# Hybrid decoder block on one core: x loaded first by SP, w_in tiles asked for at the fifth step, both copies of the transposed x on ScalarE

## The chip, the core and the metric

The kernel runs on one core of a Trainium2 chip. Its time is the device time of one execution in microseconds (us); three runs of the kernel before are given. TensorE (PE) multiplies, VectorE (DVE) and ScalarE (ACT) do elementwise work and copies out of PSUM, GpSimd (POOL) sets memory and issues a few DMAs, SyncE (SP) only issues DMAs. Each engine has one queue and works through it in order.

## The reference

One decoder block over 256 tokens of width 2048, in float32:

```
mod = silu(c) @ W_ada + b_ada            # shift1, scale1, gate1, shift2, scale2, gate2
h   = RMSNorm(x) * (1 + scale1) + shift1
u, q, k, v = split(h @ W_in)             # 1024 columns each
y_ssm = GLU(gelu(S5(u)))                 # diagonal complex state space model, 64 groups x 16 channels
y_att = dilated_attention(qk_norm(q, k), v)   # 8 heads of 128, three branches
x = x + gate1 * (concat(y_ssm, y_att) @ W_out)
h2 = RMSNorm(x) * (1 + scale2) + shift2
x = x + gate2 * ((silu(h2 @ W_gate) * (h2 @ W_up)) @ W_down)
```

Only the first part matters here: the norm of x, the modulation, h and the product with the columns of u and the first half of q.

## The kernel before

The 256 tokens are two tiles of 128. Weights come from memory in tiles of 128 x 1024 floats (512 KB), laid out on the host. The products run in two parts for accuracy: each weight tile `raw` is rounded by ScalarE to `whi` (L134), VectorE takes the rest `wlo` = raw - whi (L136), the activations are split likewise, and TensorE adds three products (L153, L630). There are six `raw` buffers and three pairs of `whi` and `wlo`. The tiles of the products follow one list, `order`; `ahead(n)` asks for tiles until n are ready, `take()` for one when none is.

The instructions of SP are issued in the order in which the program writes them. The order of the other engines is worked out by a planner: it goes by the place in the program (earlier is preferred), by priorities written into the code (`tc.high_priority`), and by its own estimate of when operands are there. What it has fixed then runs in order.

At the start three streams are written together in a loop over n (L690). `ada_stream` (L222) computes shift1 and scale1 for 256 columns at a time: a set of eight n has two modulation steps, each of which loads four tiles of W_ada (two into `raw`, two into spare buffers called `rawp`) and multiplies them on TensorE with silu(c). When a set is complete, `ada_finish` (L206) adds its parts by small matmuls and `make_h` (L606) forms h for the two column blocks and puts 10 units of work (`u_units`, L622) in a list: the product of h with two w_in tiles for u (into the accumulators `uacc`) and one for q. From n = 9 on the loop takes units from the list.

`start()` (L650) is the third stream: `x_norm` (L325) and `s5_consts` (L372). `x_norm` transposes x on TensorE through the two accumulators `uacc` (first 8 of the 16 column blocks, then the other 8), copies them to SBUF as `xT` (L340; one accumulator on ScalarE, the other on VectorE), sums squares on ScalarE (L337) and forms the root on VectorE; its result is spread over the partitions by L351. `s5_consts` is a chain of small VectorE operations (powers of the state space matrix); it needs only the small constants `smt` until its last steps, which need `bct`, loaded at n = 10. Behind it come rotations and tables (`ssm_rot`, `ssm_tables`), which `tab_step` takes in portions from n = 9 on.

The small constants and x are loaded by ScalarE's queue (L83, L86), before its first activation; SP loads all weights (L109, L248). `ahead(NHL)` with NHL = 3 asks for the first three w_in tiles at n = 8, after the loads of the third modulation step (the steps begin at n = 0, 4, 8, ..., and are counted from 0 here).

After this come the products for q, k, v with the attention and the state space model between them, W_out, and the feed-forward part, where TensorE works nearly without a break.

Of the kernel before, what the change touches and what calls it, by code (L numbers as in the profile page):

```python
# [60 lines left out]
def body(tc, sm, tabs, bc, brow, x, wada, wg2, win, wglu, wout, wgate, wup, wdown, out):  # L61
    nc = tc.nc
    V, A, PE, G, SP = nc.vector, nc.scalar, nc.tensor, nc.gpsimd, nc.sync
# [11 lines left out]
    def acc(shape, name="acc"):  # L75
        return acc_p.tile(shape, F32, name=name, tag="acc", bufs=2)

    def ms(shape, name="ms"):
        return ms_p.tile(shape, F32, name=name, tag="ms", bufs=3)
# [3 lines left out]
    A.dma_start(smt, sm)  # L83
    xt = [xp.tile([128, D], F32, name=f"x{t}", tag="x", bufs=2) for t in range(2)]
    for t in range(2):
        A.dma_start(xt[t], x[t])  # L86
    col = lambda n: smt[:, COLS[n][0]:COLS[n][1]]
    ident = col("id")
    ones = const.tile([128, 128], F32, name="ones")
# [2 lines left out]
    def rsqrt(pool_, v, n, tag):  # L92

        y = pool_.tile([128, n], F32, name="rsy" + tag)
        t = pool_.tile([128, n], F32, name="rst" + tag)
        V.tensor_scalar(out=y.bitcast(I32), in0=v.bitcast(I32), scalar1=1, scalar2=None, op0=ALU.arith_shift_right)
        V.tensor_scalar(out=y.bitcast(I32), in0=y.bitcast(I32), scalar1=-1, scalar2=0x5F3759DF, op0=ALU.mult, op1=ALU.add)
        for _ in range(3):
            V.tensor_tensor(out=t, in0=y, in1=y, op=ALU.mult)
            V.tensor_tensor(out=t, in0=t, in1=v, op=ALU.mult)  # L100
            V.tensor_scalar(out=t, in0=t, scalar1=-0.5, scalar2=1.5, op0=ALU.mult, op1=ALU.add)
            V.tensor_tensor(out=y, in0=y, in1=t, op=ALU.mult)
        return y
# [20 lines left out]
    def ahead(n, place=None):  # L124
        while len(ready) < n and order:
            raw = load(order.pop())
            if place:
                hl = place([128, 2, 2, 512], "whl", F32R)
                hi, lo = hl[:, 0], hl[:, 1]
            else:  # L130
                hi = ring.tile([128, 2, 512], F32R, name="whi", bufs=NHL)
                lo = ring.tile([128, 2, 512], F32R, name="wlo", bufs=NHL)
            with tc.high_priority(offset=HP):
                A.copy(hi, raw)  # L134
            with tc.high_priority(offset=HP2):
                V.tensor_tensor(out=lo, in0=raw, in1=hi.bitcast(F32), op=ALU.subtract)  # L136
            ready.append((hi, lo))
# [187 lines left out]
    def x_norm():  # L325

        ss1 = p1.tile([128, 2], F32, name="ss1")
        for h in range(2):
            xn = P8([128, 8, 256], f"xT{h}")
            for t in range(2):  # L330
                for i in range(2):
                    for k in range(4):
                        kc = h * 8 + i * 4 + k
                        PE.transpose(uacc[i][:, k, t * 128:(t + 1) * 128], xt[t][:, kc * 128:(kc + 1) * 128], ident)
                if h == 0:
                    junk = P8([128, D], "junk")
                    A.activation(junk, xt[t], AF.Square, accum_out=ss1[:, t:t + 1])  # L337
                    yield
            for i in range(2):
                (V.tensor_copy if i else A.copy)(xn[:, 4 * i:4 * i + 4], uacc[i])  # L340
            xnT.append(xn)
            yield
            if h == 0:
                with tc.high_priority(offset=HH):
                    V.tensor_scalar(out=ss1, in0=ss1, scalar1=1.0 / D, scalar2=EPS, op0=ALU.mult, op1=ALU.add)
                    rs1 = rsqrt(p1, ss1, 2, "a")
                    rb = ms([128, 256], "rb")
                    for t in range(2):
                        dg = T2([128, 128], "dgx")
                        V.tensor_scalar(out=dg, in0=ident, scalar1=rs1[:, t:t + 1], scalar2=None, op0=ALU.mult)  # L350
                        PE.matmul(rb[:, t * 128:t * 128 + 128], lhsT=ones, rhs=dg, start=True, stop=True)  # L351
                    A.copy(rsx, rb)
                yield
# [243 lines left out]
    uacc = [acc([128, 4, 256], f"uacc{i}") for i in range(2)]  # L597
# [44 lines left out]
    def unit():  # L642
        while units:
            try:
                next(units[0])
                return
            except StopIteration:
                units.pop(0)

    def start():  # L650
        a, b = x_norm(), s5_consts()
        while next(a, 0) is None:
            next(b, None)
            yield
        yield
        yield from b

    def tabs_early():
        yield from st_
        for m in range(NTAB):  # L660
# [4 lines left out]
            yield from ssm_tables(m)  # L665

    st_ = start()
    tab_gen = tabs_early()
    U_ = []
# [13 lines left out]
    def tab_step(budget):  # L683
        debt[0] = max(debt[0] - budget, -budget)
        if debt[0] < 0:
            c_ = next(tab_gen, None)
            debt[0] += c_ or 0.0

    work = 0.0
    for n in range(66):  # L690
        next(ada)
        if n == NBC:
            SP.dma_start(bct.rearrange("p a b c -> p (a b c)"), bc)
        if n < 9:
            next(st_)
        else:
            tab_step(TB)
        if n == 8:
            ahead(NHL)
        if n >= U0:  # L700
            work += RATE
            while work >= 1.0:
                unit()
                work -= 1.0
# [552 lines left out]
def program(arrays):  # L1257
    import concourse.bacc as bacc
    nc = bacc.Bacc("TRN2", target_bir_lowering=False, num_devices=1)
    aps = {k: nc.dram_tensor(k, v.shape, F32, kind="ExternalInput").ap() for k, v in arrays.items()}  # L1260
    out = nc.dram_tensor("out", (2, 128, D), F32, kind="ExternalOutput").ap()
    with tile.TileContext(nc) as tc:
        body(tc, out=out, **aps)
    return nc
# [8 lines left out]
```

## Time and profile before

| | |
|---|---|
| median of 3 runs | 1247.62 us (1245.65 to 1249.0) |
| profiled execution | 1249.01 us, span 1247.2 us |
| busy: TensorE, VectorE, ScalarE, GpSimd | 1195.1, 789.7, 570.5, 50.4 us |
| granted TensorE clock, mean | 0.991 |
| read from memory | 301.54 MB, 245 GB/s over the span |

Busy times are sums over one profiled execution; TensorE's are modelled, so that a busy TensorE isn't one at its peak. A wait counts only when something that ends late depends on it. Times in rows are microseconds from the start of the span.

### The profile page before, as it was taken

The page shows a single profiled execution, that of the slowest core. Times are in us where ns is not written, and L with a number is a line of the kernel's source. Part 1 is how long each engine was busy: PE and PEld are TensorE (multiplying, and loading weights), DVE is VectorE, ACT ScalarE, POOL GpSimd, SP SyncE. Part 2 cuts the span into 40 slices and gives each one's busy share as a digit, 9 for nine tenths or more (in the row PEclk, how much of TensorE's full clock was granted, in tenths as well). Part 3 has the DMA queues.
Part 4 walks back from the last instruction along what each step waited for, and adds up shares of the span by engine and source line. Part 5 has one row for each costly group of instructions (what it writes and reads, how often), then busy time and mean ns, then how long its engine had stood idle before and what let it go on. Part 6 is the DMA issues. An engine that isn't in the chain of part 4 may idle for free.

```text
span 1247.2 us, 16987 instructions
## 1 busy us (share of the span) xinstructions
PE 1195.1 (96%) x6312; PEld 954.0 (76%) x6312; DVE 789.7 (63%) x1370; ACT 570.5 (46%) x871; POOL 50.4 (4%) x90
## 2 busy tenths in 40 slices
PE   4889899999998999999999999999999999999998
PEld 2667667667798777688888888888888878888886
DVE  7964666577879988856665565565555444545544
ACT  3654574456455545544444444444444443434332
POOL 1110001121020000000000000000000000000000
PEclk9899999999999999999999999999999999999999
DMA  9879878897996899367777777777765656666662
GB/s 378 315 288 365 312 275 292 274 315 262 339 301 215 309 319 337 117 208 240 236 236 233 233 240 244 225 235 249 236 189 186 195 161 200 206 197 206 199 205 68
DMA packets 93906, 306.85 MB, mean 246 GB/s; under 512 B 18080, under 2 KB 20544, under 8 KB 93184
## 3 DMA queue, kind: packets, MB, share of 16 engines
q1 hardware_dynamic: 80784, 294.69, 70.5%
q0 software_dynamic: 11312, 6.70, 2.8%
q10 hardware_dynamic: 1728, 4.38, 0.9%
q8 instruction: 49, 0.80, 0.3%
q14 instruction: 33, 0.27, 0.1%
HBM read 301.54 MB, written 4.19 MB: 245 GB/s over the span
## 4 chain that ended last, share of the span: by engine, by line
PE 84%; DVE 8%; DMA 3%; ACT 3%; issue 1%; POOL 0%; DVEq 0%; ACTq 0%; POOLq 0%
PE ff L153 38%; PE dn L153 14%; PE qkv L153 8%; PE dnl L153 5%; PE wo L153 4%; PE ada L254 3%; PE uacc L630 2%; DVE wlo L136 2%; DMA raw<-wada 1%; PE wol L153 1%; DMA raw<-win 1%; PE y L754 1%; PE S L724 1%; ACT whi L134 1%; PE q L153 1%
## 5 line engine op out<-in xcount | busy, mean ns | idle before, releaser
L136 DVE TENSOR_TENSOR wlo<-raw,whi 128x1024 fp32r<-128x1024 f32 x365 | 446.0, 1223 | 327.1 <-ACT whi L134 325.8
L134 ACT CAST whi<-raw 128x1024 fp32r<-128x1024 f32 x365 | 384.0, 1054 | 490.9 <-PE ff L153 270.3
L153 PE MATMUL ff<-whi,h2T 128*128 128x512 f32 x1408 | 437.3, 390 | 1.6 <-ACT h2T L1066 1.0
L153 PEld LDWEIGHTS ff<-whi,h2T 128*128 128x128 f32 x1408 | 264.0, 188 | 57.8 <-ACT h2T L1066 1.9
L153 PE MATMUL ff<-wlo,h2T 128*128 128x512 f32 x704 | 274.0, 389 | 0.0
L153 PE MATMUL dn<-whi,aT 128*128 128x512 f32 x528 | 163.2, 390 | 0.0
L153 PEld LDWEIGHTS ff<-wlo,h2T 128*128 128x128 f32 x704 | 132.2, 188 | 27.1
L153 PEld LDWEIGHTS dn<-whi,aT 128*128 128x128 f32 x528 | 99.1, 188 | 21.0 <-ACT whi L134 0.2
L153 PE MATMUL qkv<-whi,hT 128*128 128x512 f32 x320 | 108.2, 405 | 0.3 <-ACT whi L134 0.3
L153 PE MATMUL dn<-wlo,aT 128*128 128x512 f32 x264 | 103.1, 391 | 0.0
L153 PEld LDWEIGHTS qkv<-whi,hT 128*128 128x128 f32 x320 | 60.6, 190 | 25.5 <-issue 7.3
L1125 DVE SCALAR_TENSOR_TENSOR gate<-raw,cs,gate 128x1024 f32<-128x1024 f32 x32 | 41.1, 1285 | 47.1 <-DMA raw<-wg 47.1
L153 PE MATMUL qkv<-wlo,hT 128*128 128x512 f32 x160 | 64.0, 400 | 2.0 <-DVE wlo L136 2.0
L630 PE MATMUL uacc<-hT,whi 128*128 128x256 f32 x256 | 53.1, 304 | 7.0 <-ACT whi L134 7.0
L153 PEld LDWEIGHTS dn<-wlo,aT 128*128 128x128 f32 x264 | 49.6, 188 | 10.8 <-issue 0.5
L153 PE MATMUL dnl<-whi,aT 128*128 128x512 f32 x176 | 54.4, 389 | 0.0
L630 PEld LDWEIGHTS uacc<-hT,whi 128*128 128x128 f32 x256 | 43.2, 207 | 13.6 <-ACT whi L134 10.0
L254 PE MATMUL ada<-raw,c 128*4 128x256 f32 (+1 forms) x496 | 50.5, 489 | 0.0
L284 DVE SCALAR_TENSOR_TENSOR gate<-raw,cs,gate 128x1024 f32<-128x1024 f32 x32 | 41.0, 1282 | 8.6 <-DMA raw<-wada 8.2
L630 PE MATMUL uacc<-hT,wlo 128*128 128x256 f32 x128 | 39.4, 308 | 5.8 <-DVE wlo L136 5.8
L153 PEld LDWEIGHTS dnl<-whi,aT 128*128 128x128 f32 x176 | 33.0, 188 | 7.0 <-DVE o L359 0.2
L153 PEld LDWEIGHTS qkv<-wlo,hT 128*128 128x128 f32 x160 | 30.4, 190 | 9.0 <-DVE wlo L136 2.4
(318 smaller groups left out, 1253.5 us busy)
## 6 DMA issues: line engine op xcount, KB each, us to landing
raw<-wada SPq DMA_DIRECT2D x130, 512.0 KB, 5.3
raw<-wgate SPq DMA_DIRECT2D x88, 512.0 KB, 4.3
raw<-wup SPq DMA_DIRECT2D x88, 512.0 KB, 4.2
raw<-wdown SPq DMA_DIRECT2D x88, 512.0 KB, 3.6
raw<-win SPq DMA_DIRECT2D x64, 512.0 KB, 5.4
raw<-wout SPq DMA_DIRECT2D x32, 512.0 KB, 4.9
raw<-wg SPq DMA_DIRECT2D x32, 512.0 KB, 4.2
rawp<-wada SPq DMA_DIRECT2D x30, 512.0 KB, 7.4
```

The source lines that it names most:

```text
L134: A.copy(hi, raw)
L136: V.tensor_tensor(out=lo, in0=raw, in1=hi.bitcast(F32), op=ALU.subtract)
L153: PE.matmul(ps[t] if type(ps) is list else ps[:, t], lhsT=lhs(a, t), rhs=w[:, j], start=first and n == 0, stop=last and n == 2)
L254: PE.matmul(ps[32 * q:32 * q + 4, 0:w], lhsT=c7[:, kc, 3 - i:7 - i], rhs=wts[t][:, j * w:(j + 1) * w], start=q not in seen, stop=n == len( ...
L284: V.scalar_tensor_tensor(out=gb, in0=wt, scalar=cs[:, k:k + 1], in1=gb, op0=ALU.mult, op1=ALU.add)
L630: PE.matmul(uacc[b][:, c], lhsT=wt[:, j, w], rhs=h[:, j, a], start=(kc == 0 and n == 0 and c % 2 == 0), stop=(kc == 15 and n == 2), skip_g ...
L724: PE.matmul(S[:, e, Q], lhsT=wv[:, 0, Q, e].rearrange("p i c -> p (i c)"), rhs=U[:, m, Q], start=True, stop=True)
L754: PE.matmul(y[:, Q], lhsT=Vt[:, Q, e].rearrange("p r c -> p (r c)"), rhs=hp[:, e, Q], start=False, stop=e == 1, skip_group_check=True)
L1125: V.scalar_tensor_tensor(out=g, in0=wt, scalar=cs[:, k:k + 1], in1=g, op0=ALU.mult, op1=ALU.add)
```

## The change

Three edits in the code before the loop and one in it. SP issues the two loads of x, ahead of everything else in its queue; ScalarE issues only the small constants. Both copies of the transposed x are on ScalarE. In `start()` the steps of `s5_consts` no longer alternate with `x_norm` throughout: two of its steps are taken at n = 0 and 1, none from n = 2 to 8, the rest from n = 9 on by `tab_step`. Before, one was taken at each n from 0 to 4 and from 6 to 8. `ahead(NHL)` stands at n = 4, behind the loads of the second modulation step.

```
     for t in range(2):
-        A.dma_start(xt[t], x[t])
+        SP.dma_start(xt[t], x[t])
...
             for i in range(2):
-                (V.tensor_copy if i else A.copy)(xn[:, 4 * i:4 * i + 4], uacc[i])
+                A.copy(xn[:, 4 * i:4 * i + 4], uacc[i])
...
     def start():
         a, b = x_norm(), s5_consts()
-        while next(a, 0) is None:
-            next(b, None)
+        for i in range(9):
+            next(a, None)
+            if i < 2:
+                next(b, None)
             yield
-        yield
         yield from b
...
-        if n == 8:
+        if n == 4:
             ahead(NHL)
```

## Rows read from the trace of the kernel before

**Rows 1.** The page's chain of work that ended last: shares by engine.
```profile
PE 84%; DVE 8%; DMA 3%; ACT 3%; issue 1%; POOL 0%; DVEq 0%; ACTq 0%; POOLq 0%
```

**Rows 2.** Windows by stage: window, busy us (instructions) per engine, clock, DMA share, GB/s.
```profile
0.00:40.00 40.00, 20.73 (x166) 14.59 (x167) 31.49 (x193) 13.88 (x24) 5.79 (x17) 0.92 0.98 385
40.00:100.00 60.00, 51.85 (x494) 38.72 (x494) 43.49 (x129) 35.79 (x84) 8.17 (x11) 0.94 0.78 283
100.00:160.00 60.00, 54.98 (x520) 40.57 (x519) 35.56 (x93) 29.02 (x58) 2.01 (x6) 1.00 0.90 347
160.00:200.00 40.00, 39.47 (x242) 27.55 (x242) 27.29 (x74) 26.20 (x68) 0.42 (x1) 1.00 0.81 289
550.00:1247.00 697.00, 692.58 (x3091) 572.27 (x3089) 376.50 (x331) 282.67 (x283) 0.00 (x0) 1.00 0.67 210
```

**Rows 3.** Timeline of TensorE, 10 to 50 us: start, length, instruction, wait before it.
```profile
15.06 1.89 PE L254 MATMUL ada<-rawp,c 128*4 128x256 f32 x16 [2.79 <-DVE ss_tb L362]
...
21.51 1.75 PE L334 MATMUL uacc<-smt,x 128*128 128x128 f32 x14 [1.32 <-DVE xT L340]
23.20 1.05 PE L254 MATMUL ada<-rawp,c 128*4 128x256 f32 x16
24.06 1.05 PE L254 MATMUL ada<-raw,c 128*4 128x256 f32 x16
...
27.93 1.05 PE L254 MATMUL ada<-raw,c 128*4 128x256 f32 x16
30.61 0.51 PE L630 MATMUL uacc<-hT,whi 128*128 128x256 f32 x2 [1.64 <-ACT whi L134]
33.98 0.58 PE L630 MATMUL uacc<-hT,wlo 128*128 128x256 f32 x1 [2.86 <-DVE wlo L136]
...
46.00 1.05 PE L254 MATMUL ada<-raw,c 128*4 128x256 f32 x16
```

**Rows 4.** Timeline of VectorE, 19 to 85 us.
```profile
20.23 1.22 DVE L340 COPY xT<-uacc 128x1024 f32<-128x1024 f32 x1 [3.20 <-PE uacc L334]
...
32.70 1.22 DVE L136 TENSOR_TENSOR wlo<-raw,whi 128x1024 fp32r<-128x1024 f32 x1
```

**Rows 5.** Windows in the first 70 us, columns as in Rows 2 (engines PE, PEld, DVE, ACT, POOL).
```profile
0.00:5.00 5.00, 0.00 (x0) 0.00 (x0) 0.89 (x5) 1.28 (x1) 3.88 (x15) 1.00 0.66 196
5.00:40.00 35.00, 20.73 (x166) 14.59 (x167) 30.60 (x188) 12.60 (x23) 1.90 (x2) 0.90 1.02 412
35.00:40.00 5.00, 5.00 (x25) 5.00 (x25) 4.74 (x12) 1.00 (x5) 0.00 (x0) 0.50 1.03 410
40.00:50.00 10.00, 8.28 (x72) 6.05 (x71) 9.65 (x29) 4.43 (x16) 1.84 (x2) 0.99 0.60 216
20.00:70.00 50.00, 39.41 (x362) 29.15 (x361) 48.43 (x202) 28.13 (x68) 4.59 (x6) 0.90 0.88 340
```

**Rows 6.** Timeline of SP's queue, 0 to 130 us.
```profile
17.86 7.20 SPq L109 DMA_DIRECT2D raw<-win  x3
...
28.98 0.90 SPq L248 DMA_DIRECT2D rawp<-wada  x2
...
37.56 9.44 SPq L109 DMA_DIRECT2D raw<-wada  x2
```

**Rows 7.** The tile x, to 60 us: ns min/median/max, first and last start.
```profile
L86 ACTq DMA_DIRECT2D x<-x x2: 354/402/450, 1.2 to 5.3; - x2
L337 ACT ACTIVATE junk<-x x2: 1910/1911/1912, 10.2 to 14.0; 128x2048 f32<-128x2048 f32 x2
...
DMA to landing us min/median/max: 8.7/8.8/9.0
```

**Rows 8.** The tile xT, to 60 us: columns as in Rows 7.
```profile
L340 ACT COPY xT<-uacc x2: 1012/1012/1012, 19.7 to 23.1; 128x1024 f32<-128x1024 f32 x2
L340 DVE COPY xT<-uacc x2: 1223/1224/1224, 20.2 to 26.4; 128x1024 f32<-128x1024 f32 x2
```

**Rows 9.** Timeline of ScalarE, 0 to 100 us.
```profile
29.53 2.92 ACT L134 CAST whi<-raw 128x1024 fp32r<-128x1024 f32 x3
```

**Rows 10.** The tile rawp, to 60 us: time to landing.
```profile
DMA to landing us min/median/max: 4.7/8.3/13.9
```

## The prediction

> **What bounds the kernel now.** I read the chain of waits first: TensorE holds 84% of it [rows 1], so time is lost or won where TensorE stands still. The windows by stage say where that is [rows 2]: of the first 40 us TensorE works 20.73, of the next 60 it works 51.85, of the 60 after that 54.98. That is 19.3 + 8.2 + 5.0 = 32.5 us of standing still in the first 160 us, against 4.4 us in the last 697. The change touches only the start, so I read the first 70 us engine by engine.
>
> TensorE [rows 3]: modulation step 0 (32 matmuls) starts at 15.06; the transposes of the second half of x's columns then wait 1.32 us for VectorE's copy of the first; step 1's matmuls stand behind them and end at 24.06 + 1.05 = 25.11, step 2's at 28.98. The first unit of u starts at 30.61, stops after two matmuls and waits 2.86 us for the low part of a w_in tile, so that it really runs from 33.98. Step 3's matmuls stand behind all the units of the first set and end at 46.00 + 1.05 = 47.05.
>
> VectorE [rows 4, 5]: idle for 3.20 us until 20.23, because the copy of uacc stands in its queue and waits for TensorE; from 20 to 70 us it is 97% busy (48.43 of 50). What it could have done at 17 us it drags behind it up to 70.
>
> DMA [rows 5, 6]: 196 GB/s in the first 5 us, then at its ceiling up to 40 us (share 1.02, 412 GB/s), then 0.60 of it up to 50. The SP queue says why: the second of the two loads issued from 37.56 could not go before 37.56 + 9.44 = 47.0, when step 3's matmuls end and free its raw buffer.
>
> **The change part by part.**
>
> *x on SP, first.* Now ScalarE issues the two tiles of x at 1.2 and 5.3 us, and each takes 8.7 to 9.0 us to land, because SP's loads share the DMA engines; the squares that wait for them start at 10.2 and 14.0 [rows 7]. Afterwards SP issues both at some 0.7 to 1.6 us with nothing of its own ahead of them. With 185 KB of small constants, 384 KB of tables and 2,048 KB of x that is 2.68 MB, 0.98 MB of them in the first 5 us and the rest at 412 GB/s: x is complete at 5 + 4.1 = 9 us instead of 14. The price is that the tiles of steps 0 and 1 stand behind 2 MB more. At the end of step 1 it is no price: the same 6,713 KB (6.87 MB) have to arrive by then in either order, 0.98 + 5.89 MB, so 5 + 14.3 = 19.3 us. SP's two more issues cost 0.35 to 0.45 us each [rows 7], hidden because the DMA engines are the ceiling; without that cover, 0.8 us.
> The Trainium skill (DMA: Bandwidth & Descriptors, section Issuing engines are not separate DMA queues) says that transfers issued by different engines end on the same 16 DMA engines and interleave, so that another issuer saves only the issue time. The share of 1.02 agrees with the sharing. By this rule alone x would come as late as now, and the 3.9 us of step 1 below would fall out of the sum: 1245, the time of the first rival; I think it counts less here, because the order of the issues changes too.
>
> *Both copies on ScalarE.* VectorE loses two copies of 1.22 us [rows 8] and the wait of 3.20: 5.6 us. ScalarE gains two copies of 1.01 us, in series where they were side by side, so each pair ends 0.8 us later than it could (2.0 against 1.2). ScalarE's squares of 1.91 us then end at about 11, the copies at 13, the second pair at 17, all before step 1's tiles at 19.3; that wait hides them. Without that cover: 0.8 us a pair, 1.6.
>
> *What is late next: step 1's matmuls.* Today they wait behind transposes that wait for VectorE; then only for their tiles: 19.3 + 1.9 (32 matmuls, 23.20 to 25.11) = 21.2 against 25.11, **3.9 us** earlier. From there to the first unit of u it is 5.5 us today (25.11 to 30.61: copy of the sums, small matmuls, g and shift, h); I leave that: 26.7.
>
> *w_in tiles at the fifth step.* Three tiles, 1.57 MB, go ahead of step 2's 2.1 MB and land by 19.3 + 3.8 = 23.1. ScalarE's casts (three in 2.92 us [rows 9]) and the first subtraction (1.22 us [rows 4]) then end by 26 to 27, so the stop from 30.61 to 33.98 goes: **3.4 us**. Bounds: 0 if the subtractions stay behind the constants in VectorE's queue, 3.4 if they come ahead of them; I take 3.4, as VectorE has 3.2 us more room. Step 2's tiles land 3.8 us later, at about 28; its matmuls end at 28.98 today, so nothing is lost while the first unit runs ahead of them.
>
> *Six steps of the state space constants* move from steps 2 to 8 to step 9 and later, and with them the rotations and tables in the order in which the planner prefers work. They need only the small constants, so VectorE still has nothing better before 20 us; I cost it at nothing. Bounds: a gain of 1 us if a subtraction that now comes before them saves TensorE another wait, a loss of 3.2 if VectorE idles as it does now.
>
> **The sum.** Two chains run through the first 70 us, and the later one counts: TensorE's first unit is 3.9 + 3.4 = 7.3 us earlier, VectorE's backlog 5.6. TensorE's small matmuls for the tables wait for VectorE, so part of the 7.3 is given back; I take the middle, 6.5. The DMA engines must follow: they idle 10 x 0.40 = 4.0 us in 40 to 50 and 60 x 0.22 = 13.2 in 40 to 100 [rows 2, 5]; with step 3's matmuls some 7 us earlier the raw buffer comes free in time and the first of these gaps closes. From 160 us TensorE's queue is nearly full (39.47 of 40 us), so the lead is carried to the end. The profiled execution took 1249.01 us, its span 1247.2 and 1.8 around it: 1249.0 - 6.5 = 1242.5. The median of the runs, 1247.62, is 1.4 below it: **1241.1 us**.
>
> **The clock.** From 35 to 40 us the granted clock is 0.50 [rows 5], after TensorE had stood from 31.1 to 33.98, so the first unit ran at 1.2 GHz. I assume the same afterwards, since TensorE stands between 21.2 and 26.7.
> The Trainium skill (TensorE: Matmul & The Clock Gate, Part 1) says that an array that idles falls to 1.2 GHz and has to be kept busy to rise again; the 0.50 after the stop agrees. By it an earlier start after a longer pause could keep the first unit slow for longer than now, and the gain would be 1 to 3 us less, an estimate inside the range.
>
> **Rivals.**
> *The lead is swallowed.* From 100 to 160 us the DMA engines are 0.90 busy at 347 GB/s [rows 2]. If the loop of buffer, load and matmul between 50 and 100 us keeps its idle time, only the gap at 45 us counts, and part of it: 2 to 3 us, 1245. For: the high share. Against: the 13.2 us of idle DMA time ahead of it, more than the lead needs. If a raw buffer holds the third early w_in load, so that the change does not do all it says, two of three still come and it ends here too. Chance 0.22.
> *The lead grows.* Casts and subtractions of the second and third set come ahead of the table work, and TensorE's 8.2 us of waits in 40 to 100 us shrink too: lead 10 to 14 us, 1237 to 1233. For: step 3's last tiles were issued by 28.98 + 0.90 [rows 6] and used after 45. Against: VectorE has the same work less 2.4 us. Chance 0.16.
> *Slower: step 2 blocks the first unit.* There are six raw buffers: four go to steps 0 and 1, so with three w_in tiles ahead, step 2's second tile needs one that step 1's matmuls free, and SP issues in order. Step 2's matmuls stand ahead of the first unit now. If they stay there, it waits for their tiles: issued from 21.2, landed 8.3 us later [rows 10], 1.9 us of matmuls, 31.4, still before 33.98. It turns into a loss when they are issued after 33.98 - 1.9 - 8.3 = 23.8. With step 1 ending at 25.11 as now it is 35.3, 1.3 us later, and a hole of some 3 us in the load stream besides, with step 3 behind it: 1247.6 + 4.3 = 1252. For: SP's third w_in load waits like this today, until 17.86 + 7.20 = 25.06 [rows 6]. Against: x is there 5 us sooner, so nothing holds step 1 so long. Chance 0.16.
>
> **How the numbers follow.** Forecast (lead of 4 to 9 us) 0.46, swallowed 0.22, grows 0.16, slower 0.16. About 0.3% (3.7 us) is what a measurement of this kernel tells from no change: faster 0.46 + 0.16 = 0.62, the same 0.22, slower 0.16. The range goes from the grown lead (1233) to most of the slower case (1251).
>
> **What would show it.** Right: the second tile of x landed by 10 us; VectorE without its wait at 17 to 20; step 1's matmuls over by 22; the first unit running from 26 to 28 without a stop for the low part; no DMA gap at 43 to 48; TensorE's work at 200 us 5 to 8 us earlier. Wrong: step 2's matmuls ahead of the first unit and it at 33 or later, or a lead at 60 us that is gone by 160.

## The result, and the profile after

The changed kernel takes 1255.86 us (median of 6 runs, 1252.96 to 1256.39), the kernel before 1247.96 beside it (6 runs). The ratio is 1.0055 [1.0039, 1.0071]: slower by 6.9 us [4.9, 8.9] (the medians lie 7.9 apart). 1241.1 was predicted, 6.5 us faster.

Where it is lost can be read from the start of the feed-forward part, which is the same work in both. From the tile `ff` (ns of one: least, median, most; first and last start), first of the kernel before, then of the changed one:

```profile
L153 PE MATMUL ff<-whi,h2T x1408: 387/389/504, 507.4 to 998.2; 128*128 128x512 f32 x176
```

```profile
L153 PE MATMUL ff<-whi,h2T x1408: 387/389/504, 514.6 to 1005.4; 128*128 128x512 f32 x176
```

It starts 7.2 us later and ends 7.2 later; the spans differ by 7.3 (1247.2 and 1254.5). The first unit of u starts 5.8 us later (30.61 in [rows 3], where it stops again until 33.98; 36.43 below, where it runs on), the last matmul of u 7.9 us later (165.4 and 173.3). So the loss is made in the first 165 us and carried on. The windows of the changed kernel, as in [rows 2]:

```profile
0.00:40.00 40.00, 17.73 (x118) 12.98 (x119) 33.21 (x200) 16.86 (x31) 5.79 (x17) 0.89 0.87 338
40.00:100.00 60.00, 50.22 (x476) 37.09 (x475) 38.15 (x112) 31.02 (x64) 5.42 (x7) 0.93 0.84 304
100.00:160.00 60.00, 52.86 (x531) 39.67 (x529) 34.66 (x98) 30.02 (x68) 4.64 (x10) 1.00 0.87 317
160.00:200.00 40.00, 39.48 (x253) 27.09 (x252) 26.53 (x71) 25.86 (x67) 0.42 (x1) 1.00 0.79 283
```

TensorE works 3.00 us less in the first stretch, 1.63 less in the second, 2.12 less in the third and the same in the fourth: 6.75 of the 7.3.

TensorE's timeline from 14 to 62 us, changed kernel, beside [rows 3]:

```profile
20.71 1.22 PE L351 MATMUL rb<-dgx,ones 128*128 128x128 f32 x4 [4.10 <-DVE dgx L350]
21.87 1.89 PE L254 MATMUL ada<-rawp,c 128*4 128x256 f32 x16
23.53 1.40 PE L254 MATMUL ada<-raw,c 128*4 128x256 f32 x16
...
25.62 1.04 PE L254 MATMUL ada<-raw,c 128*4 128x256 f32 x16
27.16 0.61 PE L211 MATMUL adac<-sel,adaev 128*128 128x2 f32 x4 [0.50 <-ACT adaev L266]
36.43 0.80 PE L630 MATMUL uacc<-hT,whi 128*128 128x256 f32 x2 [8.66 <-ACT hT L616]
42.00 1.05 PE L254 MATMUL ada<-rawp,c 128*4 128x256 f32 x16
...
58.47 0.80 PE L630 MATMUL uacc<-hT,whi 128*128 128x256 f32 x2 [4.31 <-ACT whi L134]
```

Three waits are new. `rb`, which spreads the root of x's norm, now stands ahead of step 0's matmuls; step 0, which ran at 15.06, waits behind it. Step 1 ends at 26.66 (before 25.11). The sums of the modulation are out at 27.77, but h comes 8.66 us later. And the second unit waits 4.31 us for a cast.

Why h is late stands in VectorE's timeline, 23 to 56 us:

```profile
29.60 1.29 DVE L359 TENSOR_TENSOR wkr<-te,el 128x512 f32<-128x512 f32 x2
30.93 0.76 DVE L359 TENSOR_TENSOR te<-wkr 128x256 f32<-128x256 f32 x2
31.61 2.35 DVE L136 TENSOR_TENSOR wlo<-raw,whi 128x1024 fp32r<-128x1024 f32 x2
33.88 0.15 DVE L215 TENSOR_TENSOR sh<-adac,smt 128x2 f32<-128x2 f32 x1
...
35.36 0.88 DVE L614 SCALAR_TENSOR_TENSOR htmp<-xT,g,rsx 128x256 f32<-128x256 f32 x2
```

It is hardly ever idle, but it works on the powers (`el`), the first rotation (`wkr`, `te`) and two low parts before it comes to the shift. In the trace 187 of its instructions start ahead of the shift, in the kernel before 135 (the expectations below count them in the instruction list, as 177 and 128).

What step 0's delay does to the loads: SP's queue, and windows of the changed kernel (columns as in [rows 5]).

```profile
11.27 13.63 SPq L109 DMA_DIRECT2D raw<-win  x3
25.00 1.93 SPq L109 DMA_DIRECT2D raw<-wada  x2
```

```profile
20.00:25.00 5.00, 4.29 (x44) 2.11 (x48) 5.00 (x48) 2.32 (x3) 0.00 (x0) 1.00 0.36 143
25.00:30.00 5.00, 2.27 (x36) 1.08 (x28) 4.90 (x34) 1.42 (x2) 0.00 (x0) 1.00 0.89 293
30.00:35.00 5.00, 0.00 (x0) 0.00 (x0) 4.93 (x10) 0.00 (x0) 0.00 (x0) 0.61 1.03 415
35.00:40.00 5.00, 3.57 (x14) 3.38 (x15) 4.82 (x10) 3.90 (x16) 0.00 (x0) 0.50 1.00 409
```

The third w_in load can't be issued before 11.27 + 13.63 = 24.90, when step 0's matmuls end and free its raw buffer. The DMA engines, at their ceiling there before [rows 5], fall to 0.36. TensorE does nothing from 30 to 35; the granted clock falls to 0.61 and then 0.50 (1.2 GHz), as it did before after the stop at 31. (The 1.00 of the window from 20 to 25 is not a measured clock; the last section says why.)

Of what was meant, x comes early. Tile x of the changed kernel, beside [rows 7]:

```profile
L337 ACT ACTIVATE junk<-x x2: 1894/1902/1911, 6.8 to 10.0; 128x2048 f32<-128x2048 f32 x2
...
DMA to landing us min/median/max: 5.8/7.3/8.8
```

### The profile page after: what moved, and what is told of

Same layout as the page of the kernel before. It is cut to its first block, busy times and chain, and to the rows that moved or that the text cites. A ratio compares the mean times of both kernels' runs of the same rounds, so it can differ in the third digit from the quotient of the medians.

```text
span 1254.5 us, 16980 instructions
## 1 busy us (share of the span) xinstructions
PE 1196.6 (95%) x6312; PEld 955.9 (76%) x6312; DVE 787.7 (63%) x1368; ACT 573.3 (46%) x873; POOL 50.3 (4%) x90
## 4 chain that ended last, share of the span: by engine, by line
PE 85%; DVE 6%; DMA 3%; ACT 3%; issue 1%; SPq 0%; POOL 0%; DVEq 0%; POOLq 0%; ACTq 0%
PE ff L153 38%; PE dn L153 14%; PE qkv L153 7%; PE dnl L153 5%; PE wo L153 4%; PE uacc L630 3%; PE ada L254 3%; DMA raw<-wada 2%; DVE wlo L136 1%; PE q L153 1%; PE wol L153 1%; PE y L755 1%; PE S L725 1%; PE atp L1148 1%; ACT whi L134 1%
```

## The experiments

Four theories, not exclusive: A, VectorE's fixed order holds back the shift and so the first unit. B, TensorE's fixed order (`rb` ahead of step 0) holds a raw buffer, SP and the loads. C, the small constants, on which VectorE's chain starts, come later beside x's loads. D, formed from the first twelve, the fixed start order has a loss of its own at the second unit. The numbers are those in the labels of the runs. Intervals are 95%; a difference of two ratios is good to about 0.2%. The starts of the first unit and of the last matmul of u (uacc) come from one profiled execution each, which can lie some microseconds from its kernel's median (17: 1248.32 and 1251.53; 9: 1259.77 and 1255.47); `wtp` is the tables' first transpose on TensorE. In the kernel before, in 14 and in 15 the first unit stops again, until 33.98, 33.69 and 33.17; in the others it runs on, with 0.8 us of waiting at most.

| kernel | ratio to before | first u | first wtp | last uacc |
|---|---|---|---|---|
| before | 1 | 30.6 | 48.8 | 165.4 |
| changed | 1.0055 [1.0039, 1.0071] | 36.4 | 73.4 | 173.3 |
| x on SP alone (1) | 1.0025 [1.0014, 1.0037] | 38.1 | 53.1 | 170.2 |
| w_in early alone (2) | 0.9998 [0.9983, 1.0014] | 29.9 | 47.4 | 164.2 |
| copies alone (14) | 0.9980 [0.9969, 0.9990] | 29.3 | 48.0 | 162.8 |
| start order alone (15) | 1.0034 [1.0020, 1.0047] | 29.8 | 71.0 | 169.6 |
| all but x on SP (3) | 1.0018 [1.0006, 1.0031] | 28.9 | 68.8 | 166.9 |
| all but w_in early (4) | 1.0033 [1.0021, 1.0044] | 34.6 | 69.6 | 169.1 |
| all but start order (17) | 1.0024 [1.0009, 1.0038] | 36.6 | 52.9 | 168.9 |
| copies and w_in early (18) | 1.0012 [0.9999, 1.0024] | 28.8 | 47.6 | 165.3 |
| both order edges (11) | 1.0003 [0.9991, 1.0016] | 27.9 | 65.8 | 166.5 |
| both, constants on SP (12) | 0.9989 [0.9975, 1.0004] | 27.9 | 65.5 | 164.2 |

**1 to 4: the parts.** Each is the diff above, cut to the part named, or with the part taken out.

*1.* Only `A.dma_start(xt[t], x[t])` to `SP.dma_start(xt[t], x[t])`.

> Only the loads of x go to SP, first; the other three edits are undone. Theory A (order): with x ahead of the modulation tiles in one queue the planner believes that set 0 is complete later and puts some 50 more VectorE instructions ahead of its shift and g (177 instead of 128 stand ahead of them); VectorE works through them in order, so the first unit of u starts late. It expects this edit alone to cost most of the loss: 4 to 8 us slower than before, first unit at 35 us or later. Theory B (buffer): the loss comes from the early w_in loads, the third of which holds SP until 24.9 us and empties the DMA queues; it expects this kernel to be no slower than before, within 2 us. Theory C (small constants landing 1.4 us later, behind x): 1 to 2 us slower.

1.0025, with 185 of VectorE's instructions already ahead of the shift. x on SP alone costs 3.1 us [1.7, 4.6]: the late first unit (38.1) is as A expected, the size is below its 4 to 8 us.

*2.* Only `if n == 8:` to `if n == 4:` ahead of `ahead(NHL)`.

> Only the w_in tiles are asked for at n = 4. Theory A: the order on VectorE stays (127 instructions ahead of the first shift) and the wlo subtractions come earlier, so the first unit loses its stop: 2 to 5 us faster than before. Theory B: the third w_in load waits for a raw buffer and holds SP with step 2's tiles behind it: 3 to 7 us slower, a DMA hole before 30 us. Theory C: no change.

0.9998. The stop for the low part is gone and the first unit starts at 29.9, yet the time is that of before: neither A's gain nor B's loss.

*3.* The change with `SP.dma_start(xt[t], x[t])` back to `A.dma_start`.

> All of the change but the loads of x, which ScalarE issues as before. Theory A: the loss is gone, 0 to 5 us faster than the kernel before. Theory B: the loss stays, 4 to 8 us slower than before, because the early w_in loads are in it. Theory C: the loss shrinks by 1 to 2 us only.

1.0018, which fits none of the three: x takes most of the loss with it, but something is left that isn't the early loads, which are free alone.

*4.* The change with `if n == 4:` back to `if n == 8:`.

> All of the change but the w_in tiles, which are asked for at n = 8 as before. Theory A: still 4 to 8 us slower than before, because shift and g of set 0 stand behind 176 VectorE instructions as in the changed kernel. Theory B: the loss is gone, within 2 us of before. Theory C: 1 to 2 us slower than before.

1.0033, 4.1 us [2.6, 5.5], at the lower end of A's range; B's and C's ranges are left. With x on SP the early loads seem to cost, 0.22% between the two ratios, which their intervals don't quite settle.

**5 and 10: VectorE's order (A).** In 5 the first rotation's ones are written by VectorE from a value of h, so that the rotation can't stand ahead of h; in 10 the powers `el`, on which it rests, stand behind h:

```
+        if mp == 0:
+            ts(E[:, 0, :, 0:1], hT[0][:, 0, 0, 0:8].bitcast(F32).unsqueeze(2), 0.0, 1.0, ALU.mult, ALU.add)
+        else:
+            G.memset(E[:, 0, :, 0:1], 1.0)
```

```
-        csq(el[:, 0, 0], el[:, 0, 1], th, tmpa)
+        with tc.issue_after(h0[1].ins):
+            csq(el[:, 0, 0], el[:, 0, 1], th, tmpa)
```

> The changed kernel, but the first rotation's ones are written by VectorE from h of set 0 (times 0 plus 1), so that the planner can't put rotations ahead of that set's shift and g: 158 instead of 177 instructions stand ahead of them. DMA order and buffers are those of the changed kernel. Theory A (VectorE's fixed order makes the first unit late): shift and g at 27 to 28 us instead of 33.88, first unit at 30 to 31 instead of 36.43, and 4 to 6 us less than the changed kernel in all, so 1 to 3 us slower than before. Theory B (the DMA hole at 20 to 25 us decides): first unit a little earlier, but waiting for tiles instead; within 2 us of the changed kernel.

> The changed kernel, with an edge of order on VectorE: the chain of powers el (and so all rotations) stands behind h of set 0, so that 117 instead of 177 instructions stand ahead of that set's shift and g. TensorE's order is the same, so the DMA hole stays. Theory A: shift and g right behind the small matmuls at 27.8, first unit at 30 us, 4 to 6 us less than the changed kernel. Theory B: as with the rotations alone (first unit 4.4 us earlier, 1 us of it left): 1 to 2 us less than the changed kernel, 5 us slower than before.

5: 1.0048 [1.0034, 1.0061], first unit at 32.0, no resolved gain where A expected 4 to 6 us. 10: 1.0028 [1.0017, 1.0040], first unit at 31.8, with 122 instructions ahead of the shift in the trace. The unit comes 4.6 us sooner and about half the loss goes, between what A and B expected. The two first units start within 0.2 us of each other and the ratios are 0.20% apart, so the start of the first unit alone does not set the time. The hole in the loads stays in 10:

```profile
20.00:25.00 5.00, 4.44 (x36) 2.09 (x40) 3.72 (x18) 2.36 (x3) 0.00 (x0) 0.50 0.34 136
```

**6 and 9: the buffer that step 0 holds (B).** In 6 only two w_in tiles are asked for at n = 4 and the third at n = 8. In 9 `rb` stands behind step 0's matmuls:

```
         if n == 4:
+            ahead(2)
+        if n == 8:
             ahead(NHL)
```

```
-                        PE.matmul(rb[:, t * 128:t * 128 + 128], lhsT=ones, rhs=dg, start=True, stop=True)
+                        with tc.issue_after(mm0[-1].ins):
+                            PE.matmul(rb[:, t * 128:t * 128 + 128], lhsT=ones, rhs=dg, start=True, stop=True)
```

> The changed kernel, but only two w_in tiles are asked for at n = 4 and the third at n = 8, so that SP isn't held before step 2's tiles by a buffer that step 0's matmuls free. Theory A: VectorE's order is the same (177 instructions ahead of shift and g), the first unit stays at 36 us, within 2 us of the changed kernel. Theory B: the hole in the DMA stream at 20 to 25 us closes and 3 to 5 us come back.

> The changed kernel, with one edge of order on TensorE: the two matmuls that spread the root (L351) stand behind step 0's matmuls, which in the changed kernel stand behind them and so wait for VectorE until 21.87 us although their tiles are there by about 14. VectorE's order is the same. Theory B, restated (step 0's late matmuls free a raw buffer late, SP is held until 24.9, the DMA stream has a hole at 20 to 25 us, share 0.36, that is never made up): share 0.9 or more at 20 to 25, 3 to 5 us less than the changed kernel, so 2 to 4 us slower than before. Theory A (VectorE's order): shift and g stay at 33 to 34 us, first unit at 36, less than 2 us less than the changed kernel.

6: 1.0066 [1.0050, 1.0082]. The hole that B wanted closed is still there, a DMA share of 0.34 in 20 to 25 us, because step 2's next load needs the same buffer; the time is as A expected, within 2 us of the change. 9: 1.0041 [1.0028, 1.0055]. Step 0's matmuls end at 19.2 and the hole is gone:

```profile
20.00:25.00 5.00, 2.82 (x39) 1.55 (x39) 5.00 (x48) 3.06 (x5) 0.00 (x0) 1.00 1.02 397
```

but the first unit still starts at 36.32, behind VectorE, as A expected. The hole alone is worth little (0.14%, not resolved): the unit waits 10.98 us for h there, not for tiles.

**7: the small constants (C).** `SP.dma_start(smt, sm)` ahead of x in place of `A.dma_start(smt, sm)`.

> The changed kernel, but SP issues the small constants too, ahead of x, so that no x is in their way: they should land at 4.5 to 5.3 us instead of 6.68. Theory C (everything on VectorE starts 1.4 us later and stays late): 1.4 us less than the changed kernel, first unit at 35. Theories A and B: the order is unchanged and VectorE is what decides up to 36 us, so A expects the same 1 to 1.5 us; B expects nothing.

1.0031 [1.0016, 1.0046]. They land 2.3 us after their issue, in the changed kernel 5.9, before 4.5. 0.24% better than the change, barely resolved and more than the 1.4 us expected; the first unit starts at 33.55, still behind 7.76 us of waiting for h.

**8: x early without SP.** The kernel before with the early loads, and ScalarE's three loads put ahead of all else:

```
+    with tc.high_priority(offset=200):
+        A.dma_start(smt, sm)
+        for t in range(2):
+            A.dma_start(xt[t], x[t])
```

> The kernel before with the w_in tiles at n = 4, and ScalarE issues both tiles of x before its first activation (half 1 at 1.6 us instead of 5.3). Theory A: x comes early without standing ahead of the modulation tiles in the planner's view of SP's queue, so shift and g stay early (122 instructions ahead of them): first unit at 27 to 29 us, 2 to 5 us faster than before. Theory B: as slow as the early w_in loads alone or slower, 0 to 3 us slower than before.

0.9998 [0.9987, 1.0009], as with the early loads alone; A's 2 to 5 us did not come. The second issue moves from 5.3 to 1.7 us, but the squares that wait for it start at 13.9 (14.0 in [rows 7]): x came no sooner. The Trainium skill (DMA: Bandwidth & Descriptors, section Issuing engines are not separate DMA queues) says that loads of different issuers interleave on the same DMA engines; the trace agrees, with 13.9 against 14.0. What brought x forward in the change was that SP's own loads came behind it.

**11 and 12: both edges, and the constants too.** 11 has the edges of 9 and 10, 12 also that of 7.

> The changed kernel with both edges of order. A and B as two halves of one cause: step 0's matmuls at 14 to 17 us, no DMA hole, step 1 by 23.5, first unit at 26 to 28 us, which is where the prediction had put it; then 6 to 9 us less than the changed kernel, 0 to 3 us faster than before. If the first unit comes at 27 us and the time is still 2 us or more above before, a third cause sits behind 40 us.

> As with both edges, and SP issues the small constants ahead of x, so that VectorE, ScalarE and TensorE start 1.4 us sooner. If the start bounds: 1 to 2 us less than with both edges alone, first unit at 25 to 27 us, 1 to 5 us faster than before. If the modulation tiles bound by then (step 1's land at 19 to 20 us): no further gain.

1.0003 and 0.9989. The edges alone gave 0.14% (not resolved) and 0.27%; together they give 0.52%, nearly all that the change lost, so the edge of B is worth 0.25% once that of A is there. A and B together hold nearly all of the loss, though the edges do not put the old order back: 122 of VectorE's instructions start ahead of the shift now, 135 in the kernel before. The constants on SP add 0.14% in 12, not resolved. In 11 TensorE does at the first unit what was forecast for the change: it starts at 27.88, without a stop for the low part. Then:

```profile
27.88 0.79 PE L636 MATMUL uacc<-hT,whi 128*128 128x256 f32 x2 [2.79 <-ACT hT L621]
...
50.88 0.80 PE L636 MATMUL uacc<-hT,whi 128*128 128x256 f32 x2 [4.76 <-ACT whi L134]
```

The lead over the kernel before is 2.7 us at 28 and does not last: the last uacc matmul comes at 166.5, before at 165.4. The windows from 45 to 50 us, first of the kernel before, then of 11, show where TensorE falls behind:

```profile
45.00:50.00 5.00, 3.28 (x41) 1.69 (x40) 4.65 (x18) 2.40 (x6) 0.00 (x0) 1.00 0.46 140
45.00:50.00 5.00, 1.12 (x24) 0.32 (x12) 5.00 (x16) 2.87 (x6) 0.00 (x0) 1.00 0.96 369
```

The second unit is not later in 11 (50.88, before 55.33). But while its cast and its low part are made, TensorE has the first of the tables' matmuls to do in the kernel before, and nothing in 11, where they come from 65.8 on.

**13: is it ScalarE's order there?** As 12, with the cast of the fourth w_in tile put ahead of the tables' copies:

```
+                if m < 2:
+                    edge.enter_context(tc.issue_after(casts[3].ins))
                 A.copy(wst[ps_, ...
```

> As e12_both_smt, and in the tables of the state space the six copies of wst and c0 wait in ScalarE's order until the cast of the fourth w_in tile (whi of the second unit) is out; that cast stood behind four of them and is to start right behind hT of the second unit, about 46.7 us in place of 49.8. Theory that ScalarE's fixed order takes the lead: the second unit starts at 47.5 to 48 us in place of 50.9 and the last uacc matmul is 2 to 3 us earlier than in e12_both_smt (164.2), so the ratio to the kernel before goes from 0.9989 to about 0.997. Rival, VectorE's backlog takes it anyway: the unit starts at 47.5 to 48, but then waits for wlo, which VectorE reaches about 50.5, and the last uacc matmul and the time stay within 1 us of e12_both_smt (ratio 0.998 to 1.000).

0.9976 [0.9967, 0.9986], not resolved from 12. The second unit starts as early as hoped, and stops for VectorE instead:

```profile
47.62 0.51 PE L639 MATMUL uacc<-hT,whi 128*128 128x256 f32 x2 [1.49 <-ACT whi L134]
51.02 0.58 PE L639 MATMUL uacc<-hT,wlo 128*128 128x256 f32 x1 [2.90 <-DVE wlo L136]
```

At the second unit the rival was right: 1.49 + 2.90 = 4.4 us of waiting in place of 4.76. The rest is undecided: the last uacc matmul comes at 165.4, 1.2 us later than in 12, while the ratio lies just below the rival's range and its interval takes in the 0.997 of the theory.

**14 to 16: the copies and the start order.** 14 has only the copies (`A.copy` for both), 15 only the loop in `start()`, 16 is 12 with `(V.tensor_copy if i else A.copy)` back.

> The kernel before with only the change that both copies of the transposed x stand on ScalarE. VectorE's order has 142 instructions ahead of set 0's shift in place of 128. Theory that the order ahead of the shift sets the loss: the first unit 1 to 1.5 us later than in the kernel before (30.6), ratio 1.000 to 1.002, and the copies hold most of the 0.18% left with the x line undone. Rival, the fixed start order holds it: ratio 1.000 or below, since VectorE loses a copy and a wait of 3.2 us.

> The kernel before with only the start order written as nine fixed steps. The engines' orders at the start are the same as in the kernel before, with 128 instructions ahead of the shift. Theory: ratio 1.000 within 0.1%, first unit at 30.6 within 0.5. Rival (this edit holds the 0.18%): ratio 1.001 to 1.003, with the loss later than the first unit, as the constants' steps that now come earlier in the program shift the order of the table work.

> As e12_both_smt, with the copies of the transposed x as in the kernel before (one on VectorE, one on ScalarE). Theory that the copies cost through the order only, which the two edges fix: ratio within 0.1% of e12_both_smt (0.9989). Rival, the second copy on ScalarE costs by itself: 0.997 to 0.998. Other side, VectorE is the tight engine at 15 to 40 us and a copy more there delays the shift: 1.000 to 1.001, first unit 0.5 to 1 us later than 27.9.

14: 0.9980 [0.9969, 0.9990], faster, though 149 of VectorE's instructions start ahead of the shift; its theory falls. 15: 1.0034 [1.0020, 1.0047]: a part that I had taken for free costs 4.2 us [2.5, 5.9], and its theory falls for the rival, a loss behind the first unit. 16: 0.9981 [0.9970, 0.9992], not resolved from 12: a cost of 1.000 to 1.001 is out, theory and rival are not told apart.

Where 14 gains is not at the start of the first unit, which stops again and really runs from 33.69, 0.3 us sooner than before. Its timeline there, and its window beside the 0.50 of [rows 5]:

```profile
33.69 0.58 PE L630 MATMUL uacc<-hT,wlo 128*128 128x256 f32 x1 [3.90 <-DVE wlo L136]
```

```profile
35.00:40.00 5.00, 5.00 (x37) 5.00 (x37) 4.96 (x9) 1.60 (x7) 0.00 (x0) 0.83 1.02 406
```

In these 5 us TensorE gets through 37 matmuls at a granted clock of 0.83, before through 25 at 0.50, and step 3 follows at 43.47 in place of 45.13. That is one profile of each kernel; whether the clock does so in every execution of 14 was not tested.

What 15 does is seen in the tile `wtp` and in a window; first the kernel before, then 15:

```profile
L568 PE MATMUL wtp<-smt,wst x32: 270/272/418, 48.8 to 94.7; 128*128 128x128 f32 x32
```

```profile
L568 PE MATMUL wtp<-smt,wst x20: 270/272/331, 71.0 to 94.4; 128*128 128x128 f32 x20
```

```profile
50.00:60.00 10.00, 8.79 (x85) 5.83 (x85) 9.61 (x39) 8.89 (x21) 1.37 (x2) 0.83 0.86 322
```

```profile
50.00:60.00 10.00, 5.25 (x28) 4.82 (x32) 9.83 (x39) 5.45 (x10) 0.00 (x0) 0.66 0.87 319
```

The waits of TensorE in 40 to 60 us in 15 (us in total, times, longest) name the place:

```profile
PE uacc L630 <- ACT whi L134: 4.8, 1, 4.8
```

The second unit starts at nearly the same time in both (55.33 before, 54.29 in 15). But in the kernel before TensorE's order has eight transposes and sixteen more matmuls of the tables ahead of it; in 15 they stand some 20 us later, and TensorE waits 4.83 us. It works 3.5 us less in these 10 us.

**17 and 18.** 17 is the change with the loop in `start()` as before; 18 the kernel before with the copies and the early loads.

> The whole change with the start order alone as in the kernel before. VectorE still has 177 instructions ahead of set 0's shift and TensorE still rb ahead of step 0, so the first unit stays at 35 to 36.5 us; TensorE has the tables' matmuls ahead of the second unit again. Theory that the start order carries a loss of its own at the second unit: the wait of 4.3 us for whi at 53 to 58 us goes, the last uacc matmul is 3 to 4 us earlier than 173.3, and the ratio to the kernel before is about 1.002 (1.0055 less 0.0034). Rival, that it is the same loss counted twice (the late first unit hides it): ratio 1.004 to 1.006, last uacc matmul within 1.5 us of 173.3.

> The kernel before with both copies on ScalarE and the earlier loads of w_in; x stays with ScalarE and the start order as before. Theory: VectorE loses its wait of 3.2 us, w_in's low parts are early, and the second unit keeps the order of before: first unit at 28 to 29.5 us without a stop for wlo, the last uacc matmul at 161 to 163 (before 165.4), ratio 0.996 to 0.998. Rival, the early loads add nothing to the copies: 0.998 as with the copies alone, last uacc matmul within 1 us of 162.8.

17: 1.0024 [1.0009, 1.0038], as D expected: the first unit is as late as in the change (36.6), `wtp` is back at 52.9, the wait of 4.31 us is gone and the last uacc matmul 4.4 us sooner. Inside the change the start order costs 0.31%. 18: 1.0012 [0.9999, 1.0024], a miss, slower than the copies alone. Its first unit runs from 28.79 without a stop; then SP holds two w_in loads from 44.22 to 54.65, and the DMA engines run dry:

```profile
44.22 10.43 SPq L109 DMA_DIRECT2D raw<-win  x2
```

```profile
50.00:55.00 5.00, 4.33 (x52) 1.90 (x51) 4.08 (x19) 2.90 (x6) 0.00 (x0) 0.60 0.03 11
```

The fastest kernels measured are 13, 14 and 16, each about 0.2% under the kernel before and not resolved from one another. The simplest of them is 14, one line. In 13 and 16 the last uacc matmul comes at 165.4, as before, and the first `ff` matmul at 505.0 and 504.6 in place of 507.4: they gain behind the start. From the one to the other it is 337.9 to 339.8 us in the four kernels that have the constants on SP (7, 12, 13, 16), 342.0 in the kernel before and 340.7 to 344.4 in all others but 17 (337.6, the only one whose clock does not fall to 0.50 in this stretch). What the constants on SP change there is open.

## Why the prediction was wrong

*x on SP, first.* Right in what it does: x complete by 10.0 us (the second issue at 1.2, 8.8 to land), 9 forecast. It came sooner by its place ahead of SP's own loads, for the earlier issue alone, in 8, changed nothing (13.9). Not costed: the small constants land 1.4 us later beside it (5.9 us after issue, before 4.5); putting them first gave 0.24% in 7 and 0.14% in 12, partly behind 165 us.

*Both copies on ScalarE.* Right in part: VectorE's wait of 3.20 us for the copy is gone, and alone the edit gains 2.5 us [1.2, 3.9], less than half of the 5.6 of backlog. That the gain is the backlog isn't shown: in 14 VectorE waits 2.55 us for the sums of the modulation instead, the first unit still stops for its low part, and the step forward in its profile is at the clock.

*Step 1's matmuls "only for their tiles".* This step failed first. I moved the operands and kept the order of the instructions as the kernel before had it; but the order is worked out anew. With x ahead in SP's queue the transposes of x's second half come ahead of step 0 (in 1 too), in the change `rb` with them, and on VectorE 187 instructions ahead of the shift. So step 1 ended at 26.66, not at 21.2, and the 5.5 us from there to the first unit became 9.8. With both edges step 1 ends at 23.2 and the unit starts at 27.9 (11), with the constants on SP as well at 22.6 and 27.9 (12): what I had worked out from the operands, 21.2 and 26.7, was right to 2.0 and 1.2 us. Of that, 1.4 us is the landing of step 1's last tile, at 20.7 in the change as in the kernel before, where I had summed up 19.3: not more than 2.5 of the 3.9 us were ever there. That the planner reorders because it takes the modulation's tiles for later is my reading of its order; the edges show what the order costs, not why it was chosen.

*w_in tiles at the fifth step, 3.4 us.* The stop is gone, in the change as in 2, 11 and 18, but the gain is zero by run 2. The lead doesn't reach 60 us: by then TensorE has worked 37.52 us in 2 and 37.79 in the kernel before.

*Six steps of the constants, "I cost it at nothing".* This step failed too: it costs 4.2 us [2.5, 5.9] alone, 0.31% inside the change. The bound of a loss of 3.2 us stood there, for an idle VectorE; the loss came on TensorE, whose matmuls for the tables fell behind the second unit and left it nothing to do while VectorE and ScalarE made that unit ready.

*The rivals.* "Slower" had the right sign and resource: six raw buffers, SP in order, a hole in the load stream. It had the wrong place. The first unit never waited for step 2 (its matmuls came at 42.00, in the midst of the first set's units); the third w_in load was held by step 0's buffer, and the unit waited for VectorE. Its size, 1252, was short of 1255.86: neither VectorE's order nor the start order was in it, so that the right sign is luck in part. "Swallowed" is what happens once that is mended: in 2, 8 and 11 the first unit is 0.7 to 2.7 us earlier and the ratio is 0.9998 to 1.0003.

*The clock.* As assumed: 0.50 in 35 to 40, as before. The longer pause did not keep the first unit slow for longer: it runs at 0.50 from 36.43 to 41.3, in the kernel before from 33.98 to 40.2.

Open: the parts alone sum to 0.37% (0.25 + 0.34 - 0.20 - 0.02), the whole is 0.55%; with three or four intervals of 0.13% that is not settled, and the copies and the early loads, each free or better alone, are 0.32% worse together than the copies by themselves. Run 18 shows the dry DMA engines there, but no run took that away. No run has both edges and the start order of the kernel before, which is what the waits at the second unit in 11 and 15 ask for. How much of 15's 4.2 us is the wait itself and how much the lower clock behind it (0.66 against 0.83 in 50 to 60 us) was not tested either.

## What to carry to other kernels

Where a planner writes the engines' orders, an edit that moves a load or a step in the program has the price of the whole new order, not of the moved step: read the new order at the next two points where the critical engine waits, and put edges where work that can wait has moved ahead of work that can't. Nor is work that fills a wait free to move away: TensorE's small matmuls for the tables filled a wait at 50 us, and moved to 70 us they left it empty, in a kernel 4.2 us slower. And a lead made at the start counts only as far as the work behind it is ready: in 11 and 13 a cast or a low part was not, in 18 a buffer was not free.

## What was not expected of the hardware

The first modulation matmuls after a wait run long, in windows that read a granted clock of 1.00: sixteen took 1.89 us at 21.87 in the changed kernel, behind a wait of 4.10, and sixteen like them 1.04 at 25.62. That 1.00 is not measured: the clock's entries in this trace begin at 24.3 us (at 19.7 in that of the kernel before), and a stretch without an entry is printed as 1.00. In 10 the entries begin earlier and read 0.50 from 19.3 to 26.1 (its window from 20 to 25 stands above). The same matmuls there, within that stretch and right behind it:

```profile
21.71 1.89 PE L255 MATMUL ada<-rawp,c 128*4 128x256 f32 x16
...
26.45 1.04 PE L255 MATMUL ada<-raw,c 128*4 128x256 f32 x16
```

So 1.89 and 1.04 are the two levels of the clock, 1.2 and 2.4 GHz, and the 1.89 of 15.06 in [rows 3] is most likely the lower one as well: a clock that a profile gives for the first 20 us or so has to be held against the length of a known matmul.

A small load on another engine's queue is slowed by large ones that start beside it: the 185 KB of constants took 5.9 us to land beside x and W_ada on SP, 4.5 beside W_ada on SP with x behind them in their own queue, and 2.3 as the first in SP's queue.
